# A block with RG-LRU, stick-breaking attention and a squared-ReLU MLP: half of the weight sums made on load by GpSimd, half in memory

## The chip, the cores and the metric

The kernel runs on one core of a Trainium2 chip. The metric is the time of one execution in microseconds (us) of device time, as the median of several runs. PE is TensorE with its weight loads as PEld, DVE is VectorE, ACT is ScalarE, POOL is GpSimd, SP is SyncE, which issues most DMAs.

## The reference

One block of 1024 tokens and 1024 features in float32. The change is about the weights of the MLP: `w_up` is 1024 x 4096 and `w_down` 4096 x 1024.

```python
def hybrid_mixer(h, w_in, ...):
    proj = h @ w_in
    q, k, v, xl, gl = jnp.split(proj, ...)
    q, k = rms_norm per head of 64
    attn = stick_breaking_attention(q, k, v)      # 8 heads, blocks of 128 queries
    xl = causal_depthwise_conv(xl, conv_w, conv_b)
    lru = rg_lru(xl, ...) * gelu(gl)
    return jnp.concatenate([attn, lru], axis=-1) @ w_out

def sq_relu_mlp(h, w_up, w_down):
    return jnp.square(jax.nn.relu(h @ w_up)) @ w_down

def reference(x, ...):
    h = rms_norm(x, norm1_g)
    x = x + hybrid_mixer(h, ...)
    h = rms_norm(x, norm2_g)
    x = x + sq_relu_mlp(h, w_up, w_down)
    return x
```

## The kernel before

**Halves.** Every operand of a large product is kept as two float32r halves: `split` casts the raw tile on ACT (the high part) and subtracts that from the raw tile on DVE or POOL (the low part, line 60). A product then takes three matmuls: low with high, high with low, high with high.

**Stages.** The first 158 us are the norm, the first projections and the recurrence. From 158 to 475 us the list `ORDER` interleaves attention (`A`, for pair of heads, head and block of 256 queries), the projections of the pairs (`O` loads the weights `wr_p` by SP, `I` multiplies, as `pd20` for pair 2 and tokens 0 to 127), the gate of the recurrence (`W` loads `wr_gl`, `G` multiplies) and the weight sums (`Y`). The output projection lasts to 582 us. Then come the two groups of the MLP, g = 0 and 1, each with 2048 of the 4096 hidden features. The code is written in this order, and a scheduler with a model of the engines' times places each engine's instructions before the kernel is built; the order of each engine and queue is then fixed.

**The MLP.** Up and down are each done with seven products of half-size blocks instead of eight (Strassen's scheme). One product is 96 matmuls of 512 columns. On the way up, loop `a` does two products, `s` two, `t` one and `u` two, over eight steps j; the results are the four units `U[:, j, q]`, squared after the ReLU. The way down takes the units in the products p1, p5, p6, p3, p7, p2, p4, each in four steps of 512 KB of weights (`rp`) and two units, some of them subtracted first (`s1`, `s2` on POOL, `s3` on DVE, `s4` into a raw tile). Some products need sums of two to four blocks of a weight matrix.

**The weight sums.** These are made in DRAM, by DMAs that POOL issues: `weight_sum(n)` copies a block of 2 MB or adds one to what is there, and is issued behind the last marked POOL instruction. There are 32 calls: eight for each of u0, d0 (way up and down of group 0), u1 and d1. The first sixteen are the `Y` entries of `ORDER`, the others are issued in the loops of group 0. SP loads the finished sums like any other weights, through three raw tiles of 4 KB a partition (pool `raws`).

**Load of weights in a step.** A step issues the load by SP, then ACT's cast, then the low part on DVE, or for every third one on POOL (`lo_eng`), then PE's matmuls. Stationary tiles have three buffers and moving tiles five.

## Time and profile before

| | before |
|---|---|
| median of 3 runs | 1229.58 us (1226.56 to 1234.42) |
| the profiled execution | 1226.07 us, its span 1224.3 us |
| mean granted clock of PE | 0.977 of full speed |
| PE busy | 1145.2 us, 94% of the span |
| DVE, ACT, POOL busy | 66%, 45%, 46% |
| weight sums issued | 32, the first at 158.46 us |

The span is from the first to the last instruction of the profiled execution; 1.8 us of its time lie around it. The granted clock is what the chip allowed PE, as a share of full speed. Shares of busy time are means over stages with different limits.

### The profile page before, as it was taken

To read this page: it belongs to the slowest core of one execution; us is meant where nothing else is said; L and a number is where in the kernel's file an instruction comes from. 1 tells how busy PE (TensorE), PEld (TensorE's weight loads), DVE (VectorE), ACT (ScalarE), POOL (GpSimd) and SP (SyncE) were. 2 spreads that over 40 slices of the span, in tenths; PEclk is the share of its full clock that TensorE was granted. 3 is DMA by queue.
4 is the path that set the end of the run, shared out by engine and by line. 5 is a ranking of instruction groups with operands and counts; after the bars stand their busy time and mean duration, and the time that the engine had idled before them with its cause. 6 is when DMAs were issued, how large, how long until landed. Compare 5 with 4: busy or idle time off the path is not lost.

```text
span 1224.3 us, 15029 instructions
## 1 busy us (share of the span) xinstructions
PE 1145.2 (94%) x5410; PEld 940.2 (77%) x5410; DVE 804.6 (66%) x1156; ACT 551.4 (45%) x959; POOL 561.4 (46%) x490
## 2 busy tenths in 40 slices
...
GB/s 261 49 47 35 33 162 119 212 194 110 293 105 185 64 208 140 209 1 1 154 274 105 199 240 129 255 240 181 261 63 49 138 89 93 128 109 64 172 104 69
DMA packets 92555, 169.62 MB, mean 139 GB/s; under 512 B 7697, under 2 KB 26177, under 8 KB 92481
## 3 DMA queue, kind: packets, MB, share of 16 engines
q1 hardware_dynamic: 67392, 101.56, 25.8%
q0 software_dynamic: 25088, 67.11, 23.3%
...
HBM read 158.16 MB, written 77.60 MB: 193 GB/s over the span
## 4 chain that ended last, share of the span: by engine, by line
PE 62%; DVE 14%; DMA 8%; issue 7%; POOL 6%; ACT 4%; SPq 0%; ACTq 0%; DVEq 0%; POOLq 0%
PE p L647 19%; PE pa L647 11%; PE pb L647 4%; PE pc L647 4%; DMA wr_p<-in_w_in_dram 3%; PE po L71 3%; PE po L72 2%; PE po L73 2%; DVE g L455 2%; PE pd L72 2%; PE pd L71 2%; PE pd L73 2%; PE av L475 2%; DMA rp<-in_w_down_dram 2%; PE z L446 2%
## 5 line engine op out<-in xcount | busy, mean ns | idle before, releaser
L456 POOL TENSOR_TENSOR w<-w,g 128x128 f32<-128x128 f32 (+3 forms) x96 | 104.8, 1104 | 92.5 <-DVE g L455 35.7
L60 DVE TENSOR_TENSOR ml_p<-rp,mh_p 128x1024 fp32r<-128x1024 f32 x56 | 94.5, 1687 | 74.9 <-ACT mh_p L558 74.7
L675 POOL TENSOR_TENSOR U<-U 128x512 f32<-128x512 f32 x64 | 84.6, 1373 | 74.1 <-ACT U L674 68.0
L455 DVE TENSOR_TENSOR_SCAN g<-g 128x128 f32<-128x128 f32 (+3 forms) x96 | 110.7, 1165 | 3.4 <-ACT g L450 2.3
L71 PE MATMUL pd<-wh_p,hTl 128*128 128x384 f32 x256 | 91.7, 360 | 15.2 <-ACT wh_p L178 6.9
L647 PE MATMUL pa<-mh_p,sl_p 128*128 128x512 f32 x256 | 100.8, 394 | 3.2 <-DVE sl_p L60 3.1
L558 ACT CAST sh_p<-U 128x1024 fp32r<-128x1024 f32 x48 | 50.5, 1052 | 113.5 <-PE pa L647 48.9
L647 PE MATMUL pa<-mh_p,sh_p 128*128 128x512 f32 x256 | 100.3, 392 | 0.0
L647 PE MATMUL pa<-ml_p,sh_p 128*128 128x512 f32 x256 | 100.2, 391 | 0.0
L72 PE MATMUL pd<-wl_p,hTh 128*128 128x384 f32 x256 | 91.0, 356 | 3.8 <-POOL wl_p L60 3.0
L60 POOL TENSOR_TENSOR sl_p<-U,sh_p 128x1024 fp32r<-128x1024 f32 x16 | 42.6, 2665 | 109.7 <-ACT sh_p L558 109.7
L73 PE MATMUL pd<-wh_p,hTh 128*128 128x384 f32 x256 | 88.8, 347 | 0.0
L558 ACT CAST mh_p<-rp 128x1024 fp32r<-128x1024 f32 x56 | 58.8, 1050 | 62.2 <-DMA rp<-in_w_down_dram 29.7
L60 DVE TENSOR_TENSOR sl_p<-U,sh_p 128x1024 fp32r<-128x1024 f32 x32 | 49.2, 1539 | 29.7 <-ACT sh_p L558 29.7
L71 PEld LDWEIGHTS pd<-wh_p,hTl 128*128 128x128 f32 x256 | 49.5, 194 | 20.3 <-ACT wh_p L178 7.8
L60 DVE TENSOR_TENSOR wtl<-pw,wth 128x512 fp32r<-128x512 f32 (+1 forms) x80 | 49.7, 628 | 18.5 <-ACT wth L470 17.9
L647 PEld LDWEIGHTS pa<-mh_p,sl_p 128*128 128x128 f32 x256 | 48.5, 189 | 14.8 <-DVE sl_p L60 4.4
L470 ACT CAST wth<-pw 128x512 fp32r<-128x512 f32 (+1 forms) x80 | 42.8, 546 | 33.6 <-PE pw L466 19.4
L450 ACT ACTIVATE g<-z 128x384 f32<-128x384 f32 (+3 forms) x96 | 47.7, 497 | 20.0 <-PE z L448 13.0
L647 PE MATMUL p<-mh_t,sl_s 128*128 128x512 f32 x128 | 50.5, 396 | 6.6 <-POOL sl_s L60 6.6
L647 PEld LDWEIGHTS pa<-ml_p,sh_p 128*128 128x128 f32 x256 | 48.5, 189 | 10.1
L647 PEld LDWEIGHTS pa<-mh_p,sh_p 128*128 128x128 f32 x256 | 48.4, 189 | 10.2
...
## 6 DMA issues: line engine op xcount, KB each, us to landing
...
sum_d<-in_w_down_dram POOLq DMA_DIRECT2D x12, 2048.0 KB, 14.7
...
sum_u<-sum_u POOLq DMA_DIRECT2D x4, 2048.0 KB, 18.4
...
```

The lines of the kernel that those rows point to most:

```text
L60: ins = eng.tensor_tensor(lo, src, hi.bitcast(F32), op=ALU.subtract)
L71: nc.tensor.matmul(ps, al, bh, start=start, stop=False)
L72: nc.tensor.matmul(ps, ah, bl, start=False, stop=False)
L73: nc.tensor.matmul(ps, ah, bh, start=False, stop=stop)
L446: nc.tensor.matmul(z, qT[hs, h, qr], kL[hs, k0:k0 + kn], start=False, stop=not diag)
L450: nc.scalar.activation(g[:, :kn], z, AF.Sigmoid, scale=-1.0)
L455: nc.vector.tensor_tensor_scan(gr, gr, gr, g[:, kn:kn + 1], op0=ALU.mult, op1=ALU.bypass)
L456: mark(nc.gpsimd.tensor_tensor(w[:, :kn], w[:, :kn], g[:, 1:kn + 1], op=ALU.mult))
L470: nc.scalar.copy(wth[:, :nw], pw[:, :nw])
L558: nc.scalar.copy(hl[0], src)
L647: nc.tensor.matmul(ps, x_, y_, start=start and n == 0, stop=stop and n == 2, skip_group_check=True)
L675: mark(nc.gpsimd.tensor_tensor(c, c, c, op=ALU.mult))
```

## The change

Each group now has four calls of `weight_sum` for the way up and four for the way down, 16 in place of 32: two copies, then two adds, which leave two sums of two blocks in DRAM. The rest is summed after the load: loops `s` and `u` and the products p5, p6 and p4 load two tiles of raw weights or sums, and POOL adds them (`r + q`) ahead of the split. So `u` loads 1 MB of weights a step, and p5, p6 and p4 1 MB. The low parts in these loops all go to DVE (before, every third to POOL); half of the `s1` and `s2` subtractions go from POOL to DVE; the squares of loop `u` go from POOL to ACT. The scratch of the dynamic DMAs (the ring in which the descriptors of POOL's DMAs stand) is given as 4096 where it was 16384 by default, and `raws` has six buffers in place of three. In `ORDER` there are eight `Y` entries in place of sixteen.

```diff
...
@@ -130,35 +130,21 @@
-    sums = {("u", g): dram.tile([4, 8, P, 512], F32, name=f"sum_u{g}") for g in range(2)}
-    sums.update({("d", g): dram.tile([4, 8 * P, 512], F32, name=f"sum_d{g}") for g in range(2)})
+    sums = {("u", g): dram.tile([2, 8, P, 512], F32, name=f"sum_u{g}") for g in range(2)}
+    sums.update({("d", g): dram.tile([2, 8 * P, 512], F32, name=f"sum_d{g}") for g in range(2)})
     def weight_sum(n):
-        m, g = (("u", 0), ("d", 0), ("u", 1), ("d", 1))[n // 8]
-
...
-        dst, src, adds = ((2, block(*first), False), (0, block(*other), False), (2, block(*second), True), (1, block(*first), False),
-                          (3, block(*corner), False), (0, v[2], True), (1, block(*other), True), (3, v[0], True))[n % 8]
+        m, g = (("u", 0), ("d", 0), ("u", 1), ("d", 1))[n // 4]
+        i, k, dst = ((1, 0, 0), (0, 1, 1), (0, 0, 0), (1, 1, 1))[n % 4] if m == "u" else ((1, 1, 0), (0, 0, 1), (0, 1, 0), (1, 0, 1))[n % 4]
+
+        def rows(w):
+            return w.rearrange("j p c -> (j p) c") if len(w.shape) == 3 else w
+
+
+        f = 16 * g + 8 * i
+        src = rows(w_up[k, f:f + 8] if m == "u" else w_down[k, f * P:(f + 8) * P])
         with tc.issue_after(marked[0]):
-            if adds:
-                nc.gpsimd.dma_start(v[dst], src, accum_op=ALU.add, max_dma_last_dim=2048)
-            else:
-                nc.gpsimd.dma_start(v[dst], src, max_dma_last_dim=2048)
+            nc.gpsimd.dma_start(rows(sums[m, g][dst]), src, max_dma_last_dim=2048, **({"accum_op": ALU.add} if n % 4 > 1 else {}))
...
@@ -540,7 +526,7 @@
     xp1 = pool(ctx, "x1")
     x1 = xp1.tile([P, NT, D], F32, name="x1")
     h2 = xp1.tile([P, KC, S], F32, name="h2")
-    rwp = pool(ctx, "raws", bufs=3)
+    rwp = pool(ctx, "raws", bufs=6)
     mvp = pool(ctx, "moving", bufs=5)
     stp = pool(ctx, "stationary", bufs=3)
...
@@ -669,10 +655,13 @@
         def two(w):
             return w.rearrange("a p c -> p a c")
-        def relu2(j, q, src=None, scale=1.0):
+        def relu2(j, q, src=None, scale=1.0, pool=True):
             c = U[:, j, q]
             nc.scalar.activation(c, c if src is None else src, AF.Relu, scale=scale)
-            mark(nc.gpsimd.tensor_tensor(c, c, c, op=ALU.mult))
+            if pool:
+                mark(nc.gpsimd.tensor_tensor(c, c, c, op=ALU.mult))
+            else:
+                nc.scalar.activation(c, c, AF.Square)
...
@@ -690,8 +679,6 @@
                 ps, st = held
                 mm4(ps, st, 1, b21, False)
                 relu2(j - 1, 0, ps)
-                if g == 0 and j % 2 == 0:
-                    weight_sum(15 + j // 2)
             held = cur
         for u in range(2):
@@ -705,7 +692,13 @@
             nc.vector.tensor_tensor(r, hb(1, 1, u), hb(0, 0, u), **sub)
             t3.append(split(lo_eng(), pair(mvp, f"t3{g}{u}"), r))
         for j in range(8):
-            st = station(f"s{g}{j}", two(SU[0:2, j]))
+            r = raw(f"rs{g}{j}")
+            nc.sync.dma_start(r[:, 0], w_up[1, 16 * g + 8 + j])
+            nc.sync.dma_start(r[:, 1], SU[0, j])
+            mark(nc.gpsimd.tensor_tensor(r[:, 0], r[:, 0], r[:, 1], **add))
+            if g == 0 and j % 4 == 0:
+                weight_sum(8 + j // 4)
+            st = split(nc.vector, pair(stp, f"s{g}{j}"), r)
             ps = out_bank(f"p6_{g}{j}")
             mm4(ps, st, 0, t2)
             nc.vector.tensor_tensor(U[:, j, 2], U[:, j, 2], ps, **sub)
@@ -719,14 +712,14 @@
             nc.vector.tensor_tensor(r, hb(1, 0, u), hb(1, 1, u), **sub)
             t4.append(split(lo_eng(), pair(mvp, f"t4{g}{u}"), r))
         for j in range(8):
+            if g == 0 and j % 4 == 2:
+                weight_sum(10 + j // 4)
             if j % 2 == 0:
                 st = station(f"t{g}{j}", two(w_up[1, 16 * g + 8 + j:16 * g + 10 + j]))
             ps = out_bank(f"p4_{g}{j}")
             mm4(ps, st, j % 2, t4)
             nc.vector.tensor_tensor(U[:, j, 1], ps, U[:, j, 3], **sub)
             relu2(j, 1)
-            if g == 0 and j % 2 == 0:
-                weight_sum(20 + j // 2)
         t1 = moving("t1", [hb(0, 1, u) for u in range(2)])
         for u in range(2):
@@ -736,17 +729,23 @@
         for j in range(9):
             cur = None
             if j < 8:
-                st = station(f"u{g}{j}", two(SU[2:4, j]))
+                r, q = raw(f"ru{g}{j}"), raw(f"rv{g}{j}")
+                nc.sync.dma_start(r[:, 0], w_up[0, 16 * g + 8 + j])
+                nc.sync.dma_start(q[:, 0], w_up[1, 16 * g + 8 + j])
+                nc.sync.dma_start(r[:, 1], SU[1, j])
+                nc.sync.dma_start(q[:, 1], SU[0, j])
+                mark(nc.gpsimd.tensor_tensor(r, r, q, **add))
+                st = split(nc.vector, pair(stp, f"u{g}{j}"), r)
                 ps = out_bank(f"p5_{g}{j}")
                 mm4(ps, st, 0, t1)
                 nc.vector.tensor_tensor(U[:, j, 3], ps, U[:, j, 3], **add)
-                relu2(j, 3, scale=-1.0)
+                relu2(j, 3, scale=-1.0, pool=False)
                 cur = (ps, st)
             if held is not None:
                 ps, st = held
                 mm4(ps, st, 1, b22, False)
                 nc.vector.tensor_tensor(U[:, j - 1, 2], ps, U[:, j - 1, 2], **add)
-                relu2(j - 1, 2)
+                relu2(j - 1, 2, pool=False)
             held = cur
...
@@ -761,11 +760,15 @@
             for k in range(0, 8, 2):
                 r = raw(f"r{name}{g}{k}")
-                nc.sync.dma_start(r, src(k))
+                nc.sync.dma_start(r, src[0](k))
+                if len(src) > 1:
+                    q = raw(f"q{name}{g}{k}")
+                    nc.sync.dma_start(q, src[1](k))
+                    mark(nc.gpsimd.tensor_tensor(r, r, q, **add))
+                    if g == 0 and name != "p4" and k % 4 == 0:
+                        weight_sum(12 + (2 if name == "p6" else 0) + k // 4)
                 mv = split(nc.vector, pair(mvp, f"{name}{g}{k}"), r)
-                st = split(lo_eng(), pair(stp, f"{name}{g}{k}"), unit(k))
-                if g == 0 and k % 4 == 2 and name in steps:
-                    weight_sum(24 + 2 * steps.index(name) + k // 4)
+                st = split(nc.vector if len(src) > 1 else lo_eng(), pair(stp, f"{name}{g}{k}"), unit(k))
...
@@ -794,12 +797,12 @@
         def s1(k):
             u = U[:, k:k + 2]
-            mark(nc.gpsimd.tensor_tensor(u[:, :, 2], u[:, :, 2], u[:, :, 3], **sub))
+            (nc.gpsimd, nc.vector)[k // 2 % 2].tensor_tensor(u[:, :, 2], u[:, :, 2], u[:, :, 3], **sub)
             return u[:, :, 2]
         def s2(k):
             u = U[:, k:k + 2]
-            mark(nc.gpsimd.tensor_tensor(u[:, :, 2], u[:, :, 2], u[:, :, 0], **sub))
+            (nc.gpsimd, nc.vector)[k // 2 % 2].tensor_tensor(u[:, :, 2], u[:, :, 2], u[:, :, 0], **sub)
             return u[:, :, 2]
...
@@ -813,23 +816,22 @@
             nc.vector.scalar_tensor_tensor(u[:, :, 2], u[:, :, 2], -1.0, u[:, :, 3], op0=ALU.mult, op1=ALU.subtract)
             return u[:, :, 2]
-        steps = ("p5", "p6", "p3", "p7")
         pa = banks4(QA, "pa")
-        product("p1", pa, wd(0, 0), unit(0), True)
+        product("p1", pa, (wd(0, 0),), unit(0), True)
         acc(pa, 0, 0, rs2)
         pb = banks4(QB, "pb")
-        product("p5", pb, rd(2), s1, True)
+        product("p5", pb, (wd(0, 0), wd(0, 1)), s1, True)
         acc(pb, 1, 1, rs2)
-        product("p6", pa, rd(0), s2, False)
+        product("p6", pa, (rd(0), wd(0, 0)), s2, False)
         acc(pa, 0, 1, nrs2)
-        product("p3", pb, wd(1, 1), s4, False)
+        product("p3", pb, (wd(1, 1),), s4, False)
         acc(pb, 0, 1, rs2, True)
-        product("p7", pa, rd(1), s3, False)
+        product("p7", pa, (rd(0),), s3, False)
         acc(pa, 1, 1, nrs2, True)
         pc = banks4(QB, "pc")
-        product("p2", pc, wd(1, 0), unit(1), True)
+        product("p2", pc, (wd(1, 0),), unit(1), True)
         acc(pc, 0, 0, rs2, True)
-        product("p4", pa, rd(3), unit(3), False)
+        product("p4", pa, (rd(0), rd(1)), unit(3), False)
         acc(pa, 1, 0, rs2, True)
     for g in range(2):
@@ -849,7 +851,7 @@
     from concourse import mybir as _mybir
     from concourse.bass_utils import run_bass_kernel_spmd as _run
-    nc = _bacc.Bacc("TRN2", target_bir_lowering=False, num_devices=1)
+    nc = _bacc.Bacc("TRN2", target_bir_lowering=False, num_devices=1, dynamic_dma_scratch_size=4096)
     arrays, args = {}, []
     for name in _INS:
         a = _np.asarray(inputs[name])
```

**PE, behind the gate's last product of the first pair.** `pgl11` is the gate, `pd20` the projection of pair 2, `av` and `pw` are attention, `z` its scores. Before:

```order
L71 MATMUL pgl11_3139<-hTh_100,wl_gl0_7_2833 128x512
L72 MATMUL pgl11_3139<-hTl_101,wh_gl0_7_2832 128x512
L73 MATMUL pgl11_3139<-hTh_100,wh_gl0_7_2832 128x512
L71 MATMUL pd20_3225<-wh_p2_0_3173,hTl_101 128x384
L72 MATMUL pd20_3225<-wl_p2_0_3174,hTh_100 128x384
L73 MATMUL pd20_3225<-wh_p2_0_3173,hTh_100 128x384
```

After, the rows behind the gate:

```order
L71 MATMUL pgl11_3134<-hTh_100,wl_gl0_7_2829 128x512
L72 MATMUL pgl11_3134<-hTl_101,wh_gl0_7_2828 128x512
L73 MATMUL pgl11_3134<-hTh_100,wh_gl0_7_2828 128x512
L461 MATMUL av013_1799<-wtl0132_1832,vv0_289 128x256
L461 MATMUL av013_1799<-wth0132_1831,vv0_289 128x256
L461 MATMUL av013_1799<-wtl0132_1832,vv0_289 128x256
L461 MATMUL av013_1799<-wth0132_1831,vv0_289 128x256
L452 MATMUL pw0110_1879<-ident_79,w0120_1857 128x128
L452 MATMUL pw0110_1879<-ident_79,w0130_1868 128x128
```

The projection of pair 2 has moved some 80 rows back; attention stands in its place.

**POOL, around the low parts of pair 3's weights in the attention stretch.** `wl_p3` are these, `sum_d0` the sums for the way down of group 0, `kl`, `raw`, `w` and `g` belong to projection and attention. Before:

```order
L161 DMA sum_d0_95<-in_w_down_dram 1024x512 x2
L228 TENSOR_TENSOR raw22_3567<-raw22_3567,qkg_280 128x2x128
L449 MEMSET g2110_3380 128x1
L60 TENSOR_TENSOR wl_p3_0_3951<-wr_p3_0_3949,wh_p3_0_3950 128x384
L456 TENSOR_TENSOR w2000_3330<-w2000_3330,g2000_3329 128x128
L456 TENSOR_TENSOR w2010_3341<-w2010_3341,g2010_3340 128x256
L449 MEMSET g2120_3514 128x1
L60 TENSOR_TENSOR wl_p3_2_3963<-wr_p3_2_3961,wh_p3_2_3962 128x384
L449 MEMSET g2130_3525 128x1
L159 DMA sum_d0_95<-in_w_down_dram 1024x512
L60 TENSOR_TENSOR kl22_3646<-raw22_3567,ks22_3645 128x128 x2
L161 DMA sum_d0_95<-in_w_down_dram 1024x512
```

After:

```order
L442 TENSOR_TENSOR w2100_3365<-w2100_3365,g2100_3364 128x128
L435 MEMSET g204512_3666 128x1
L442 TENSOR_TENSOR w2110_3376<-w2110_3376,g2110_3375 128x256
L214 TENSOR_TENSOR raw22_3561<-raw22_3561,qkg_280 128x2x128
L60 TENSOR_TENSOR wl_p3_0_3944<-wr_p3_0_3942,wh_p3_0_3943 128x384
L60 TENSOR_TENSOR wl_p3_2_3956<-wr_p3_2_3954,wh_p3_2_3955 128x384
L60 TENSOR_TENSOR kl22_3640<-raw22_3561,ks22_3639 128x128 x2
L147 DMA sum_d0_95<-in_w_down_dram 1024x512
L60 TENSOR_TENSOR wl_p3_4_3968<-wr_p3_4_3966,wh_p3_4_3967 128x384
L60 TENSOR_TENSOR wl_p3_6_3980<-wr_p3_6_3978,wh_p3_6_3979 128x384
```

Where two copies, an adding sum and a further copy (and one more behind) stood within these rows, there is one adding sum; the copies that it follows stand 15 and 25 rows ahead of it.

**POOL, end of loop `u` of group 0.** `U` of 128x512 is a square, `U` of 128x2x512 the subtraction `s1`, `sl_` a low part, `ru` and `rp5` raw tiles to which a second one is added. Before:

```order
L675 TENSOR_TENSOR U_6157<-U_6157 128x512 x4
L60 TENSOR_TENSOR sl_u04_7070<-ru04_7067,sh_u04_7069 128x1024
L675 TENSOR_TENSOR U_6157<-U_6157 128x512 x2
L797 TENSOR_TENSOR U_6157<-U_6157 128x2x512
L675 TENSOR_TENSOR U_6157<-U_6157 128x512 x4
L797 TENSOR_TENSOR U_6157<-U_6157 128x2x512
L60 TENSOR_TENSOR sl_u07_7181<-ru07_7178,sh_u07_7180 128x1024
L675 TENSOR_TENSOR U_6157<-U_6157 128x512 x3
L797 TENSOR_TENSOR U_6157<-U_6157 128x2x512
L675 TENSOR_TENSOR U_6157<-U_6157 128x512 x2
```

After:

```order
L662 TENSOR_TENSOR U_6149<-U_6149 128x512 x2
L737 TENSOR_TENSOR ru05_7133<-ru05_7133,rv05_7134 128x1024
L737 TENSOR_TENSOR ru06_7175<-ru06_7175,rv06_7176 128x1024
L800 TENSOR_TENSOR U_6149<-U_6149 128x2x512
L737 TENSOR_TENSOR ru07_7217<-ru07_7217,rv07_7218 128x1024
L767 TENSOR_TENSOR rp500_7422<-rp500_7422,qp500_7424 128x1024
L147 DMA sum_d1_96<-in_w_down_dram 1024x512
L60 TENSOR_TENSOR sl_p100_7285<-U_6149,sh_p100_7284 128x1024
L800 TENSOR_TENSOR U_6149<-U_6149 128x2x512
L767 TENSOR_TENSOR rp502_7461<-rp502_7461,qp502_7463 128x1024
```

The squares are gone, and each step's add stands there; the first add for p5 stands ahead of the first low part of p1.

## Rows read from the trace of the kernel before

**Rows 1.** The page, the two DMA queues that carry data, with packets, MB and the time of the packets as a share of 16 engines over the span. q1 is the queue of SyncE's DMAs, q0 that of GpSimd's.
```profile
q1 hardware_dynamic: 67392, 101.56, 25.8%
q0 software_dynamic: 25088, 67.11, 23.3%
```

**Rows 2.** Busy time in stretches, of the matmuls of the MLP (line 647) alone. Columns: the stretch, its length, busy time of PE and of its weight loads with their instructions, the granted clock of PE, the busy share of the 16 DMA engines (all queues), GB/s. In pairs: the whole MLP of group 0 and of group 1; then by stage, group 0 ahead of group 1: the two products of loop `s`; loop `u` with p1 of the way down; p3 with p7.
```profile
581.87:913.91 332.04, 313.69 (x1345) 256.21 (x1346) 0.97 0.70 192
913.91:1220.16 306.25, 305.23 (x1345) 251.96 (x1343) 1.00 0.31 100
627.99:679.93 51.94, 45.29 (x194) 37.04 (x193) 0.93 0.55 174
958.69:1002.21 43.52, 43.52 (x193) 36.04 (x192) 1.00 0.39 126
701.69:777.81 76.12, 68.39 (x289) 54.86 (x288) 0.98 0.78 196
1023.97:1089.60 65.63, 65.58 (x289) 53.99 (x288) 1.00 0.32 105
...
821.33:870.39 49.06, 45.72 (x194) 37.03 (x192) 0.97 0.87 214
1133.12:1176.64 43.52, 43.52 (x194) 36.04 (x192) 1.00 0.44 148
```

**Rows 3.** What PE waited for in the MLP of group 0 (the four largest but one). Columns: us in total, times, longest.
```profile
PE p L647 <- POOL sl_s L60: 6.6, 1, 6.6
...
PE p L647 <- DVE sl_u L60: 2.4, 1, 2.4
PE p L647 <- POOL sl_u L60: 2.3, 1, 2.3
PE p L647 <- DVE U L742: 1.8, 1, 1.8
```

**Rows 4.** Busy time in stretches, whole engines: the attention stretch from the first sum on, and three pieces of it. Columns: stretch, length, busy time (instructions) of PE, weight loads, DVE, ACT, POOL; granted clock, DMA share, GB/s.
```profile
158.46:475.00 316.54, 288.07 (x1584) 232.96 (x1583) 267.15 (x472) 181.04 (x437) 176.06 (x235) 0.96 0.66 166
220.00:240.00 20.00, 13.46 (x71) 10.56 (x70) 12.49 (x18) 7.20 (x19) 8.32 (x10) 0.91 0.77 245
320.00:340.00 20.00, 11.55 (x45) 9.06 (x43) 9.64 (x19) 5.15 (x14) 6.36 (x8) 0.66 1.09 282
400.00:420.00 20.00, 17.01 (x70) 11.46 (x69) 13.62 (x28) 10.15 (x24) 8.46 (x15) 0.83 0.24 55
```

**Rows 5.** What PE waited for in the attention stretch: the three rows that lead to weights. Columns as in rows 3.
```profile
PE pd L71 <- ACT wh_p L178: 6.9, 2, 5.4
PE pd L72 <- POOL wl_p L60: 3.0, 1, 3.0
...
PE pgl L71 <- POOL wl_gl L60: 1.1, 2, 0.9
```

**Rows 6.** The chain that ended last, its three pieces on weight loads in this stretch. Columns: start, length, what.
```profile
223.33 10.02 DMA wr_p<-in_w_in_dram
...
310.59 21.54 DMA wr_p<-in_w_in_dram
...
391.84 11.82 DMA wr_gl<-in_w_in_dram
```

**Rows 7.** POOL around one weight load: the first two and the last of the five sums that it issued between 302.67 and 317.21 us. Columns: start, length, engine, line, operation.
```profile
302.67 1.57 POOL L161 DMA_DIRECT2D sum_d<-in_w_down_dram  x2
...
317.21 1.30 POOL L161 DMA_DIRECT2D sum_d<-in_w_down_dram  x1
```

**Rows 8.** Two tiles over the whole run: `sum_d` (what POOL spends on issuing a copy, ns min/median/max; us from issue to landing of the tile's DMAs, the SyncE loads from it among them), then `rp`, the raw tiles of the way down (cast, subtraction, us to landing of their 512 KB).
```profile
L161 POOL DMA_DIRECT2D sum_d<-in_w_down_dram x8: 757/796/1350, 302.7 to 812.6; - x8
...
DMA to landing us min/median/max: 3.6/14.7/34.2
L558 ACT CAST mh_p<-rp x56: 1038/1051/1057, 736.8 to 1194.2; 128x1024 fp32r<-128x1024 f32 x56
L60 DVE TENSOR_TENSOR ml_p<-rp,mh_p x56: 1207/1225/4701, 737.9 to 1195.2; 128x1024 fp32r<-128x1024 f32 x56
...
DMA to landing us min/median/max: 3.6/5.0/8.9
```

**Rows 9.** Groups of one line, operation and shape in the MLP, on POOL and ACT. Columns: out<-in shapes, count, busy us, mean ns of one, idle time before and what ended it.
```profile
L675 POOL TENSOR_TENSOR U<-U 128x512 f32<-128x512 f32 x64 | 84.6, 1373 | 74.1 <-ACT U L674 68.0 <-issue 6.0
...
L802 POOL TENSOR_TENSOR U<-U 128x1024 f32<-128x1024 f32 x8 | 25.6, 3198 | 7.9 <-DVE sl_p L60 7.8
...
L808 POOL TENSOR_TENSOR s<-U 128x1024 f32<-128x1024 f32 x8 | 19.2, 2402 | 31.5 <-DVE ml_p L60 23.6 <-DVE sl_p L60 7.8
...
L674 ACT ACTIVATE U<-U 128x512 f32<-128x512 f32 x48 | 29.8, 628 | 47.1 <-DVE U L742 24.1 <-DVE U L726 20.5 <-DVE U L748 2.5
```

**Rows 10.** POOL, then DVE, at the end of loop `u` of group 0. Columns as in rows 7.
```profile
716.30 4.54 POOL L675 TENSOR_TENSOR U<-U 128x512 f32<-128x512 f32 x4
720.30 2.83 POOL L60 TENSOR_TENSOR sl_u<-ru,sh_u 128x1024 fp32r<-128x1024 f32 x1
722.61 2.50 POOL L675 TENSOR_TENSOR U<-U 128x512 f32<-128x512 f32 x2
724.61 2.82 POOL L797 TENSOR_TENSOR U<-U 128x1024 f32<-128x1024 f32 x1
...
719.34 9.18 DVE L60 TENSOR_TENSOR sl_u<-ru,sh_u 128x1024 fp32r<-128x1024 f32 x1 [0.44 <-ACT sh_u L558]
```

12 lines of the change are left out of this document (removed), and 6 rows, old and new, of the table ORDER.

## The prediction

> **What bounds the kernel now.** I read the DMA queues on the page first, then the stretches of TensorE (PE) by stage, then what PE and the chain wait for, and last the prices of the elementwise operations. On the page the two data queues hold the 16 engines 25.8% and 23.3% of the span; at a span of 1224.3 us the 32 weight sums of q0 cost 285 us of all 16 engines [rows 1].
>
> The MLP tells the cost of the sums without a model, since its two groups compute the same with the same instructions, and sums are in flight only in the first. Group 0 takes 332.04 us and group 1 306.25, in which PE is busy for 305.23 at full clock: that is its floor [rows 2]. Of the 25.8 us between them, 8.4 lie in loop `s` (51.94 against 43.52), 10.5 in loop `u` with p1 (76.12 against 65.63), 5.5 in p3 with p7 (49.06 against 43.52): 24.4 in stages that read weights while sums run. In each of them the granted clock of group 0 is under 1 where group 1 has 1.00: a gap is paid once as a wait and once more as a stretch at the lower clock. The gaps end on splits of weights that came late: 6.6 us on `sl_s`, 2.4 and 2.3 on `sl_u` [rows 3].
>
> The attention stretch, from the first sum at 158.46 on, has no twin to compare with. Its chain goes three times through a weight load, of 10.02, 21.54 and 11.82 us [rows 6], and PE waits 6.9, 3.0 and 1.1 us for splits of such weights [rows 5]. Just ahead of the longest, POOL had issued five sums between 302.67 and 317.21 without being held up by the ring of its DMAs, at about 0.8 to 1.6 us a row [rows 7]. But DVE, not PE alone, has to get through this stretch: outside the three pieces it is busy for 267.15 - 35.75 = 231.4 of 256.5 us, 90% [rows 4].
>
> **Fewer sums, attention stretch.** Eight sums stand here instead of sixteen. From above: in the three pieces PE is busy for 42.0 of 60 us, against (288.07 - 42.02)/256.5 = 96% elsewhere, so 15.5 us are lost, and the clocks of 0.91, 0.66 and 0.83 cost about 20 x (0.09 + 0.34 + 0.17) = 12 more: 27. By DVE: 35.75 of 60 us against 54.1 at its 90%: 18.4 that it could do in that time and did not; what PE gains beyond it, DVE can't follow. From below: the three waits of PE, 11 us in sum [rows 5], less some 3 that the new order may cost: 8. I take 18.4, since DVE is the fuller one, less 2: an adding sum now stands behind its own copy on POOL and waits for its landing (14.7 us is the median of the tile, of copies, adds and loads [rows 8]), and the products `w` of the attention queue behind it; between copy and add stand 15 rows of POOL work, more than that landing, so the wait is short. **-16.** The move of in_proj(2) on PE (the first order in the part on the change) costs nothing by itself: PE has the attention's matmuls instead, and 80 rows later its weights have landed. The second order shows the loads of pair 3 with one adding sum behind them where five sums were.
>
> **Fewer sums, MLP group 0.** Eight remain of sixteen, four for u1 and four for d1. All 24.4 us go if what remains hides behind the run-ahead; in proportion to the sums, half stays, 12.2. Behind six raw tiles the loads are issued earlier than behind three, and there are never more than two sums at once, so I take the end near nothing: 3 stay. **-21.4.** Loads themselves grow: 1 MB per j in `u` instead of 0.5, and two tiles a step in p5, p6 and p4. A 512 KB load lands in 3.6 us from issue without sums, 8.9 at most beside them [rows 8], against a step of 5.44 us (four steps a product of 21.76; a product is half of the 43.52 us of rows 2), with three pairs in flight; group 1's loops have a DMA share of 0.32 to 0.44 [rows 2], so doubling the weights in `u` is covered there.
>
> **The adds on POOL.** Per group 8 of 128x512 in `s`, 8 of 128x1024 in `u`, 12 in p5, p6 and p4. Each waits for two loads; behind it on POOL stand the squares of the loop before and the next adds, and ACT's cast and DVE's split of the weights wait for it. POOL's price for 128x1024 is 2.40 us where it has the ports to itself (line 808, mean 2402 ns) and 3.2 among DVE's work (line 802); DVE's is 1.22 (median of the `rp` split), half of it [rows 8, 9]. In exchange POOL gives up 16 squares of 1.37 us in `u`, its third of the splits and half of the s1/s2 subtractions, and half of the issues of sums (0.8 us each for a copy [rows 8]). The squares go to ACT: 0.63 us each [rows 9]; ACT then has a cast of 1.05 and four of these, 3.6 us a step of 5.44: free.
>
> What matters is that the two engines hold each other up: in loop `u` a DVE split took 9.18 us while POOL worked off 12.7 us of its queue (4.54, 2.83, 2.50, 2.82), and PE waited 2.4 us for `sl_u` [rows 3, 10]. So I add up unshared durations of both as if they took turns. p5 before: 4 x 2.40 (s1) + 4 x 1.22 (splits of weights) + four splits of units, a third of them on POOL (2.67 x 1.22 + 1.33 x 2.40 = 6.5) = 21.0 us of 21.76. After: 4 x 2.40 (adds) + 2 x 2.40 + 2 x 1.22 (s1) + 8 x 1.22 = 26.6. That is 4.8 over for p5 and the same for p6: 9.7 a group, 19.4 in all. Loop `u` is about level (16 squares of 1.37 = 21.9 give way to 8 adds, 19.2 alone and 25.6 beside DVE); p4 goes from 4.9 + 6.5 = 11.4 to 19.4. The run-ahead can cover an excess if it starts early: p1 ahead of p5, with 11.4 of 21.76, has 10.4 us free, and the third order shows the first add of p5 ahead of p1's first split on POOL. So most of 9.7 is covered: in group 0 it is in the 3 that stay, in group 1 I give back **+3**.
>
> The rule that speaks most against this part is in the Trainium skill, "SBUF — State Buffer", "SBUF: two separate sides": GpSimd and a VectorE operation with two SBUF inputs hold the shared ports in turns, each for a whole instruction, and "GPSIMD Engine Reference", 4.1, advises VectorE for two-input elementwise work, at half the time. The trace agrees on both (9.18 us for one of 1.22 us behind a row of POOL's; 2.40 against 1.22). By that rule alone, without the run-ahead, the sum would be that of the first rival.
>
> **Sum.** -16 - 21.4 + 3 = -34.4. The profiled execution took 1226.07 us (1224.3 and 1.8 around the span), 3.5 under the median of the three runs: 1191.7 and 3.5 make **1195 us**. Its own range: 27 instead of 16 gives 1184; 8 instead, and a few us more of the 12.2 left, 1208.
>
> **Rivals.** *The ports give it back:* p5 and p6 run at their 26.6 us in both groups: 19.4 instead of the some 6 allowed, 1209. For it: p5 filled 21.0 of 21.76 already; against: p1's room. *Attention gains nothing:* the gaps move to other places, because DVE at 90% sets the pace and the new order is another draw of the scheduler: 16 back, 1211. Both together: 1225. *The small ring:* the change doesn't do what it says of the sums. A quarter of the scratch holds a quarter of the descriptors, and POOL might stand at a second sum until the first has drained; with the large one no such hold is seen [rows 7], and nothing of before shows the small. If each of the 8 adds holds POOL for 10 us, and a third to a half of that reaches PE, it is some 30 us: 1225.
>
> *Slower: POOL's queue starves DVE.* In the order, POOL ends loop `u` of group 0 with adds of 128x1024 in a row, s1 and p5's first add among them, without a square or a PSUM wait between (third order). If DVE's split is caught behind such a row as at 719.34, PE loses what it lost there: 2.4 + 2.3 and 1.8 for U (the last a wait on DVE's next step [rows 3]) and 76.12 x 0.02 = 1.5 by the clock, 8 us. There are four places a group for it (end of `u`, p5, p6, p4), 8 in all: 64 us, 1195 - 6 + 64 = 1253. It turns the result round from the sixth such place on (40.4 / 8 = 5.05).
>
> **How the numbers follow.** Forecast 0.50; ports 0.14; attention 0.12; both 0.06; ring 0.08; starved DVE 0.10. The best of all bounds is 1229.6 - 27 - 24.4 = 1178; the range 1178 to 1224 leaves out the starved DVE and the worse half of the 1225s. A measurement of this kernel tells about 1% from no change, 12.3 us; under 1217.3 are the forecast and nearly all of the two rivals at 1209 and 1211: 0.73; within 1%, both together, the ring and the edges: 0.17; above 1241.9: 0.10.
>
> **What the profile after would show.** Right: loops `s`, `u` and p3 with p7 of group 0 within 3 us of group 1's; q0 at about 12% of 16 engines; no weight load of over 10 us in the attention chain, DVE as busy there in a shorter stretch. Ports: p5 and p6 over 21.76 us in both groups, PE waiting for `ml_p` or `sl_p`, splits of DVE at 3 us and more. Ring: POOL's issues of sums at ten us instead of 0.8 to 1.6. Starved DVE: splits of 5 us and more beside rows of POOL adds, each followed by a PE gap and a stretch at the lower clock. I am wrong outright if group 1, which no sum disturbs, comes out longer than 306 us by more than the ports' 10.

## The result, and the profile after

The changed kernel takes 1215.47 us in the median of four runs (1213.39 to 1218.14), the kernel before 1228.74 beside it: a ratio of 0.9886 (0.9845 to 0.9928). It gained 13.3 us where 34 were forecast. The profiled execution of the changed kernel took 1218.14 us, its span 1216.4, 7.9 less than before; the stages below are compared on the two profiled executions.

The page after: what the data queues carried, as in [rows 1].

```profile
q1 hardware_dynamic: 79040, 122.54, 30.5%
q0 software_dynamic: 12544, 33.56, 11.8%
```

The sums take half of what they took (11.8% of 16 engines, 12 were forecast), and the loads 21 MB more. The MLP of the changed kernel by stretches, of its matmuls alone, columns as in [rows 2]. In pairs, group 0 ahead of group 1: the whole MLP; loop `s`; loop `u` with p1 as there, but p5 and p6 too; p3 with p7.

```profile
566.29:899.01 332.72, 314.79 (x1345) 257.30 (x1345) 0.97 0.58 172
899.01:1212.39 313.38, 307.99 (x1345) 252.78 (x1343) 0.99 0.38 127
613.64:657.16 43.52, 43.52 (x194) 36.05 (x193) 1.00 0.50 160
944.08:987.60 43.52, 43.52 (x194) 36.05 (x193) 1.00 0.36 116
678.92:811.97 133.05, 116.03 (x482) 93.43 (x480) 0.94 0.80 219
1009.36:1125.19 115.83, 111.61 (x482) 90.92 (x480) 0.99 0.42 140
811.97:855.49 43.52, 43.52 (x194) 36.05 (x192) 1.00 0.50 170
1125.19:1168.71 43.52, 43.52 (x194) 36.04 (x192) 1.00 0.55 190
```

Three things are to be read here. The MLP starts at 566.29 us instead of 581.87, 15.6 earlier: that is the attention term. Loop `s`, and p3 with p7, of group 0 now take 43.52 us each, as in group 1, at full clock, as forecast. But group 0 as a whole is no shorter (332.72 against 332.04), because loop `u` to p6 takes 133.05 us where five products at 21.76 take 108.8; and group 1 is 7.1 longer, all of it in the same stretch (115.83). So -15.6 + 0.7 + 7.1 = -7.8.

What PE waited for in the MLP of group 0 (columns as in [rows 3]):

```profile
PE p L633 <- DVE sl_u L60: 8.0, 2, 5.6
PE pa L633 <- DVE sl_p L60: 6.8, 1, 6.8
PE p L633 <- DVE sl_a L60: 4.0, 1, 4.0
```

The waits for `sl_s` are gone, those for `sl_u` have grown from 4.7 to 8.0 us, and one of 6.8 for p6's units (`sl_p`) is new. In the attention stretch, whole engines (columns as in [rows 4], same stretch):

```profile
158.46:475.00 316.54, 298.86 (x1622) 245.69 (x1621) 275.60 (x478) 190.07 (x447) 177.60 (x231) 0.93 0.46 126
```

PE is busy 10.8 us longer in these 316.54 us than before, with 1622 instructions against 1584. Part of that is a lower granted clock, 0.93 against 0.96, so the clock that the prediction's bound of 27 counted as lost did not come back. DVE is busy 8.5 us longer (275.60 against 267.15), 87% instead of 84%. The weight loads are no longer in the list of PE's waits, and the longest one in the chain takes 3.81 us.

POOL of the changed kernel in loop `u` and in p5 of group 0 (columns as in [rows 7], with the idle time before and its cause in brackets), then one row of DVE:

```profile
675.68 1.35 POOL L147 DMA_DIRECT2D sum_u<-in_w_up_dram  x1
...
696.56 1.30 POOL L147 DMA_DIRECT2D sum_u<-in_w_up_dram  x1 [8.83 <-issue]
697.38 2.54 POOL L662 TENSOR_TENSOR U<-U 128x512 f32<-128x512 f32 x2
699.38 5.17 POOL L737 TENSOR_TENSOR ru<-ru,rv 128x1024 f32<-128x1024 f32 x2
704.05 2.79 POOL L800 TENSOR_TENSOR U<-U 128x1024 f32<-128x1024 f32 x1
...
761.68 1.32 POOL L147 DMA_DIRECT2D sum_d<-in_w_down_dram  x1
...
780.98 1.31 POOL L147 DMA_DIRECT2D sum_d<-in_w_down_dram  x1 [12.19 <-issue]
```
```profile
698.13 9.80 DVE L60 TENSOR_TENSOR sl_u<-ru,sh_u 128x1024 fp32r<-128x1024 f32 x1 [0.44 <-ACT sh_u L544]
```

Two rivals of the prediction stand in these rows at once. POOL stood 8.83 and 12.19 us at a second adding sum (the first of each pair had landed 20.6 and 19.0 us after its issue, 0.3 us ahead of the second): the small ring. And right behind the first hold POOL works off what had queued up, 9.5 us of rows without a gap, while a split of DVE takes 9.80 us: the starved DVE.

The kernel before has the same sequence in loop `u` of group 0, with the large ring. POOL's row in [rows 10] starts right behind this issue:

```profile
715.50 1.30 POOL L159 DMA_DIRECT2D sum_u<-sum_u  x1 [8.39 <-issue]
```

This add reads a sum that an earlier add, issued at 693.77, had to complete, and that one landed at 714.78: a hold by the data, as far as the rows show, and not by the ring. So POOL could stand behind a sum before as well, outside the stretch of [rows 7]. In both kernels the row that starves DVE is work that piled up on POOL behind a hold.

### The profile page after: what moved, and what is told of

It is laid out like the page before. It is cut to its first block, busy times and chain, and to the rows that moved or that the text cites. A ratio compares the mean times of both kernels' runs of the same rounds, so it can differ in the third digit from the quotient of the medians.

```text
span 1216.4 us, 15273 instructions
## 1 busy us (share of the span) xinstructions
PE 1150.6 (95%) x5410; PEld 948.0 (78%) x5410; DVE 897.3 (74%) x1182; ACT 568.5 (47%) x991; POOL 586.5 (48%) x472
## 3 DMA queue, kind: packets, MB, share of 16 engines
q0 software_dynamic: 12544, 33.56, 11.8%
## 4 chain that ended last, share of the span: by engine, by line
PE 69%; DVE 13%; issue 8%; DMA 3%; POOL 3%; ACT 3%; SPq 0%; DVEq 0%; ACTq 0%; POOLq 0%
PE p L633 22%; PE pa L633 11%; PE pb L633 5%; PE pc L633 4%; PE pd L71 3%; PE pd L72 3%; PE pd L73 3%; PE po L71 3%; PE po L72 2%; PE po L73 2%; PE av L461 2%; PE z L432 2%; PE pw L452 2%; DVE g L441 2%; DVE sl_u L60 2%
## 5 line engine op out<-in xcount | busy, mean ns | idle before, releaser
L442 POOL TENSOR_TENSOR w<-w,g 128x128 f32<-128x128 f32 (+3 forms) x96 | 99.7, 1044 | 107.7 <-DVE g L441 52.7
L60 DVE TENSOR_TENSOR ml_p<-rp,mh_p 128x1024 fp32r<-128x1024 f32 x56 | 110.3, 1971 | 28.1 <-ACT mh_p L544 28.1
L767 POOL TENSOR_TENSOR rp<-rp,qp 128x1024 f32<-128x1024 f32 x24 | 69.0, 2876 | 70.3 <-DMA qp<-in_w_down_dram 39.8
L60 DVE TENSOR_TENSOR sl_p<-U,sh_p 128x1024 fp32r<-128x1024 f32 x38 | 63.4, 1668 | 30.7 <-ACT sh_p L544 30.7
L737 POOL TENSOR_TENSOR ru<-ru,rv 128x1024 f32<-128x1024 f32 x16 | 43.8, 2769 | 58.9 <-DMA rv<-sum_u 58.8
L662 POOL TENSOR_TENSOR U<-U 128x512 f32<-128x512 f32 x32 | 47.0, 1501 | 32.0 <-ACT U L660 32.0
L436 ACT ACTIVATE g<-z 128x384 f32<-128x384 f32 (+3 forms) x96 | 47.8, 497 | 22.9 <-PE z L434 10.4
L660 ACT ACTIVATE U<-U 128x512 f32<-128x512 f32 x48 | 30.0, 628 | 58.6 <-DVE U L721 31.1
## 6 DMA issues: line engine op xcount, KB each, us to landing
sum_d<-in_w_down_dram POOLq DMA_DIRECT2D x8, 2048.0 KB, 13.3
```

The lines of the kernel that those rows point to most:

```text
L60: ins = eng.tensor_tensor(lo, src, hi.bitcast(F32), op=ALU.subtract)
L436: nc.scalar.activation(g[:, :kn], z, AF.Sigmoid, scale=-1.0)
L442: mark(nc.gpsimd.tensor_tensor(w[:, :kn], w[:, :kn], g[:, 1:kn + 1], op=ALU.mult))
L662: mark(nc.gpsimd.tensor_tensor(c, c, c, op=ALU.mult))
L737: mark(nc.gpsimd.tensor_tensor(r, r, q, **add))
L767: mark(nc.gpsimd.tensor_tensor(r, r, q, **add))
```

## The experiments

Stages are compared by how far they exceed 21.76 us a product (worked out from the starts of their matmuls, `u` up to the first matmul of p1); a group has 14 products, so its floor is 304.6. The last column is the median where there were rounds, else the one run, the profiled one. All other columns are of one execution each.

How much chance is in one execution can be read from the table. Thirteen of these kernels, all but the two of before, the one with no sums at all and the last row, have the same instructions in the same order on PE, DVE, ACT and POOL through the attention stretch, and yet their MLP starts anywhere from 560.4 to 566.7. So up to 6 us of a difference in "MLP starts", and with it in the span, are not the edit's.

| kernel | MLP starts | group 0 | `u` | p5, p6 | `u` of group 1 | p5 of group 1 | span | us |
|---|---|---|---|---|---|---|---|---|
| before | 581.9 | 332.0 | 9.8 | 0, 0 | 0 | 0 | 1224.3 | 1228.7 |
| changed | 566.3 | 332.7 | 12.1 | 1.2, 8.8 | 2.3 | 3.9 | 1216.4 | 1215.5 |
| no sums of group 1 | 562.3 | 322.4 | 9.2 | 3.6, 0.1 | 2.5 | 3.7 | 1202.4 | 1204.2 |
| no sums at all | 554.2 | 319.7 | 8.0 | 3.6, 0.1 | 2.5 | 3.5 | 1191.5 | 1194.1 |
| sums of an eighth | 565.3 | 322.7 | 7.2 | 0, 0 | 2.4 | 3.7 | 1205.6 | 1207.3 |
| ring 8192, five raw tiles | 561.0 | 333.8 | 14.0 | 2.8, 8.0 | 4.6 | 3.9 | 1215.7 | 1220.0 |
| five raw tiles | 566.1 | 335.9 | 12.6 | 2.9, 10.7 | 0.5 | 1.9 | 1217.5 | 1219.5 |
| before, ring and tiles as changed | 594.4 | 331.8 | 20.4 | 0.2, 0.1 | 0 | 0 | 1236.6 | 1238.5 |
| sums spaced | 562.4 | 329.6 | 9.1 | 3.6, 0.1 | 2.4 | 4.2 | 1210.1 | 1211.8 |
| spaced, ACT's order | 562.1 | 325.6 | 2.8 | 4.2, 0 | 0.8 | 3.8 | 1204.3 | 1206.1 |
| changed, ACT's order | 560.4 | 330.9 | 13.6 | 1.2, 0.9 | 0.9 | 4.2 | 1208.1 | 1209.9 |
| spaced, adds on DVE | 561.4 | 328.7 | 8.9 | 0, 0 | 6.6 | 0 | 1207.8 | 1212.0 |
| spaced, both | 561.0 | 326.5 | 7.9 | 0.2, 0.2 | 5.4 | 0 | 1203.5 | 1208.9 |
| changed, adds of the way down on DVE | 566.7 | 327.1 | 11.8 | 2.7, 3.3 | 2.3 | 0 | 1207.4 | 1209.2 |
| all that helped | 560.4 | 308.4 | 0 | 0.5, 0.5 | 3.7 | 0.4 | 1186.3 | **1186.7** |
| the same, without ACT's order | 562.6 | 316.6 | 8.0 | 0, 0.6 | 7.2 | 0 | 1200.4 | 1202.2 |
| all that helped, first sums earlier | 573.6 | 307.6 | 0 | 0, 0.5 | 1.2 | 0 | 1196.1 | 1199.9 |

### Is it the sums that are left?

No sums of group 1 (group 1 reads those of group 0):

```diff
+    sums["u", 1], sums["d", 1] = sums["u", 0], sums["d", 0]
     def weight_sum(n):
+        if n >= 8:
+            return
```

> The changed kernel without the eight sums that are issued in the MLP; group 1 loads the sums of group 0 instead, so its result is another. The lower bound of what sums cost there. Ring and traffic theory: group 0 comes down to group 1's 313.4 us and the 2 to 3 us of its start, 315 to 318; 1199 to 1202 in all. Port theory: group 0 stays above 325 us, 1208 or more.

1204.22 us. Its MLP, group 0, columns as above:

```profile
562.28:884.64 322.36, 310.90 (x1345) 255.10 (x1345) 0.98 0.39 126
```

This lies between the two theories. The eight sums that run beside group 0 cost it 10.4 us (332.72 less 322.36). Even so 18 us over the floor stay, 9.2 of them in loop `u`, with no sum in flight. Is it their bytes, or that POOL has to issue them? The same number of issues, an eighth of the rows (both groups read group 0's sums):

```diff
-            nc.gpsimd.dma_start(rows(sums[m, g][dst]), src, max_dma_last_dim=2048, **({"accum_op": ALU.add} if n % 4 > 1 else {}))
+            few = slice(0, 1024 if n < 8 else 128)
+            nc.gpsimd.dma_start(rows(sums[m, g][dst])[few], src[few], max_dma_last_dim=2048, **({"accum_op": ALU.add} if n % 4 > 1 else {}))
...
-        SU = sums["u", g]
+        SU = sums["u", 0]
...
-        SD = sums["d", g]
+        SD = sums["d", 0]
```

> The changed kernel with the eight sums of group 1 at their places but an eighth of their size (256 KB in place of 2 MB); both groups load the sums of group 0, so the result is another. POOL issues as many DMAs as in the changed kernel, and the engines move an eighth. If bytes make the 10.4 us that these sums cost in group 0 (332.7 against 322.4 without them), group 0 takes 321 to 324 us. If it is the issues on POOL and the order around them, 329 to 334.

```profile
565.28:888.01 322.73, 311.59 (x1344) 255.83 (x1345) 0.98 0.41 132
```

1207.34 us, and group 0 as long as without the sums: it is their size (bytes, and with them the time the ring is held), not the issue of one. And with no sum at all:

```diff
     def weight_sum(n):
+        return
...
-        SU = sums["u", g]
+        SU = [w_up[i, 16 * g:16 * g + 8] for i in range(2)]
...
-        SD = sums["d", g]
+        SD = [w_down[i, 2048 * g + 1024:2048 * g + 2048] for i in range(2)]
...
```

> The changed kernel without any weight sum; raw blocks of the weights are loaded in their place, so the result is another. It tells what is left to gain in the attention stretch. Theory that DVE sets the pace there: the MLP starts within 4 us of where it starts with eight sums (562.3 to 566.3 us in the runs so far), since the sums are hidden. Theory that the sums still cost by half of what sixteen did: it starts 10 us or more earlier, at 552 or less. The MLP as in e3_nosum1, group 0 at 322 us.

1194.07 us. The MLP starts at 554.19, 27.7 us ahead of before: more than the 18.4 read from DVE, and in size the bound of 27 which the prediction had read from PE in its three pieces. In substance it is not that bound, which counted some 12 us for the clock: from 158.46 to 475 us the granted clock is 0.96 without any sum, as it was before. Whole engines in this kernel's attention stretch:

```profile
155.00:450.00 295.00, 283.02 (x1596) 232.54 (x1595) 261.90 (x476) 182.44 (x443) 158.62 (x220) 0.97 0.22 70
```

DVE is busy for 89%, about the 90% of the prediction; in the changed kernel it is busy for 261.08 us of the same stretch. The eight sums that stay there cost 6 to 12 us by this (the kernels with them start the MLP at 560.4 to 566.7). But this is one execution, and without the sums the scheduler also placed the attention's instructions in another order, as it did from before to the changed kernel. What the order and what the sums do was not separated.

### Is it the ring?

Twice the ring, with one raw tile less to make room for it; and the raw tile alone:

```diff
-    rwp = pool(ctx, "raws", bufs=6)
+    rwp = pool(ctx, "raws", bufs=5)
...
-    nc = _bacc.Bacc("TRN2", target_bir_lowering=False, num_devices=1, dynamic_dma_scratch_size=4096)
+    nc = _bacc.Bacc("TRN2", target_bir_lowering=False, num_devices=1, dynamic_dma_scratch_size=8192)
```

> The changed kernel with a scratch of 8192 for the dynamic DMAs, and five raw tiles in place of six to make room for it. In the changed kernel two adding sums of group 1 stand on POOL behind the landing of the one before (idle for 8.8 and 12.2 us), and loop u and product p6 of group 0 are 12.1 and 8.8 us longer than their matmuls. Ring theory: the small scratch makes POOL hold, the two holds go and with them most of this excess; group 0 takes 316 to 321 us in place of 332.7, the kernel about 1200. Port theory: POOL's adds block DVE whatever the ring does; the excess stays within 3 us, about 1215. Traffic theory: the sums in flight delay the loads of raw tiles; two adding sums now overlap, so the excess stays or grows, 1213 to 1220.

1219.99 us, ratio to before 0.9939 (0.991 to 0.9967). No issue of a sum in the MLP is held any more, and loop `u` and p6 still lose 14.0 and 8.0. DVE at the end of its loop `t`, beside 9.4 us of POOL rows from 667.96 on:

```profile
668.35 10.72 DVE L60 TENSOR_TENSOR sl_u<-ru,sh_u 128x1024 fp32r<-128x1024 f32 x1 [0.53 <-DMA ru<-sum_u]
```

> The changed kernel with five raw tiles in place of six and the scratch left at 4096: the control for the run with 8192. Ring and port theory: the holds and the excess stay, group 0 at 331 to 335 us, 1213 to 1219 in all. Traffic theory: a shorter run-ahead makes late loads later, group 0 335 us or more.

1219.49 us, one run. The two kernels have the same instructions in the same order through the whole MLP. With the larger ring group 0 is 2.1 us shorter (333.8 against 335.9), and group 1, where no sum is in flight in either, is 5.3 longer; so the 2.1 can't be told from nothing, and the times are alike too. This bounds less than it seems, as the control holds POOL for only 5.38 and 3.13 us, not for 8.83 and 12.19: what holds of that length cost the changed kernel is not shown. The subtraction that p6's units wait for there stands right behind the one of 12.19 us.

With the larger ring p6 is late without a hold. Among what its units need is a subtraction on POOL, beside operations of DVE without a break:

```profile
767.04 7.85 POOL L805 TENSOR_TENSOR U<-U 128x1024 f32<-128x1024 f32 x1 [1.26 <-DVE sl_p L60]
```

The same subtraction takes 2.40 us at 753.97. With five tiles and the small ring it takes 7.86, and p6 loses 10.7. What the small ring does to the 32 sums of before is another matter:

```diff
-    rwp = pool(ctx, "raws", bufs=3)
+    rwp = pool(ctx, "raws", bufs=6)
...
-    nc = _bacc.Bacc("TRN2", target_bir_lowering=False, num_devices=1)
+    nc = _bacc.Bacc("TRN2", target_bir_lowering=False, num_devices=1, dynamic_dma_scratch_size=4096)
```

> The kernel before with only the memory part of the change: scratch 4096 and six raw tiles, all 32 sums in DRAM as before. Ring theory: POOL, which issued five sums in 15 us with the large scratch, has to stand behind landings; some holds of 5 us and more, and the kernel at 1235 or slower. Theory that the holds are hidden and the traffic of the sums counts alone: 1220 to 1230, loop s and u of group 0 as long as before (8.4 and 9.8 us of excess) or, with more raw tiles, some us shorter.

1238.45 us, one run, its span 12.3 over before's; the MLP starts 12.5 later and is as long as before. One of POOL's holds, and the longest wait of PE in the attention stretch, then in group 0:

```profile
334.72 0.77 POOL L161 DMA_DIRECT2D sum_d<-in_w_down_dram  x1 [10.59 <-issue]
```
```profile
PE pd L72 <- POOL wl_p L60: 17.0, 1, 17.0
...
PE p L647 <- POOL sl_u L60: 13.6, 2, 11.1
```

Here low parts of weights stand behind the held sum on POOL (`wl_p` follows it by 2.7 us), and PE waits; six raw tiles don't make up for it.

### A wait that no rival had: ACT's order

Sums spaced, so that none is called in `u`, p5 or p6 (the edits in loops `a`, `s`, `t` and in the products, in this order). POOL runs ahead of PE, though, and issued the first copy for the way down, called in p3, at 767.02, with PE in p5:

```diff
+                if g == 0 and j in (1, 4):
+                    weight_sum(8 + j // 4)
...
-            if g == 0 and j % 4 == 0:
-                weight_sum(8 + j // 4)
+            if g == 0 and j == 2:
+                weight_sum(10)
...
-            if g == 0 and j % 4 == 2:
-                weight_sum(10 + j // 4)
+            if g == 0 and j == 0:
+                weight_sum(11)
...
-                    if g == 0 and name != "p4" and k % 4 == 0:
-                        weight_sum(12 + (2 if name == "p6" else 0) + k // 4)
...
+                if g == 0 and (name, k) in later:
+                    weight_sum(12 + later.index((name, k)))
...
+        later = (("p3", 0), ("p3", 4), ("p7", 4), ("p2", 4))
```

> The changed kernel, scratch 4096 and six raw tiles, with the eight sums of group 1 issued elsewhere: the copies for the way up in loop a and its adds in loop s and ahead of loop t, those for the way down in p3, p7 and p2, so that none stands in loop u, p5 or p6, where two tiles are loaded a step. Ring theory: no hold of over 3 us on POOL in these three stages; u and p6 of group 0 keep 2 to 4 us of excess as in group 1 (2.3 and 0), group 0 316 to 320 us, about 1200. Traffic theory: the same, 1200. Port theory: the excess of u and p6 stays, 1213 to 1217.

1211.78 us, ratio 0.9862 (0.9824 to 0.9901). p6 is clean and loop `u` still loses 9.1; 8.6 are now lost in `s`, p7 and p2 (2.6, 1.6 and 4.4), beside the sums that were moved there. The kernel with no sums loses 8.0 in `u`, so what does PE wait for in it? Its ACT in loop `u` of group 0, and the longest wait of PE in that group:

```profile
688.53 1.04 ACT L545 CAST mh_p<-rp 128x1024 fp32r<-128x1024 f32 x1 [7.03 <-DMA rp<-in_w_down_dram]
689.48 1.04 ACT L545 CAST sh_u<-ru 128x1024 fp32r<-128x1024 f32 x1
```
```profile
PE p L634 <- DVE sl_u L60: 5.9, 1, 5.9
```

ACT stands 7.03 us at the cast of p1's first weights (`mh_p`), with a cast of loop `u` behind it in its queue. The weights of p1 need a raw tile, and the six hold three pairs of `u`, which come free only as `u` goes on; the cast of `u` behind it then follows without a wait, so its own weights were there. If that is it, queueing p1's cast behind `u`'s last one removes it (the first line stands in loop `u`, behind its split; `casts` holds the split's cast):

```diff
+                ucast[:] = casts
...
-                mv = split(nc.vector, pair(mvp, f"{name}{g}{k}"), r)
+                with tc.issue_after(ucast[0]):
+                    mv = split(nc.vector, pair(mvp, f"{name}{g}{k}"), r)
```

> e2_spaced with one thing added: the casts of p1's weights are queued on ACT behind the last cast of loop u. In the run without the sums of group 1, ACT stood 7.8 us at p1's first cast, whose load had no free raw tile until late, with the cast of u's seventh step behind it. Queue theory: this order makes the long gap of loop u in group 0; its excess falls from 9.1 us to 2 to 4, 1203 to 1206 in all. Port theory: the excess stays at 8 us or more, 1210.

1206.14 us: loop `u` of group 0 goes from 9.1 to 2.8 over, that of group 1 from 2.4 to 0.8. Group 0 as a whole gains 4.0, as p1, p5 and `s` lose a little more. The same edit on the changed kernel as it stands:

> The changed kernel with only the casts of p1 queued on ACT behind those of loop u; sums and adds as they are in it. If the queue made u's 12.1 us of excess there too, it falls to 2 to 4 us and the kernel to 1206 to 1209. If in this kernel it is the adding sums in u (POOL held, then a row of POOL work with a DVE split of 9.8 us behind it), the excess stays at 8 us or more.

1209.85 us, but loop `u` of group 0 keeps 13.6: there the adding sum in the loop, with the late loads and the starved split that go with it, is enough by itself. The loss of p6 (8.8, now 0.9) has moved to p1, which loses 7.7 instead of 2.1, and group 0 is only 1.8 shorter; most of what the span gained, 5.9 of 8.3, lies ahead of the MLP, where the two kernels are alike. Loop `u` is 9.2 over without the sums but with the old order, and 2.8 with the sums spaced and the new order: two causes lie on one another, and either alone keeps PE waiting.

### Who should add?

The adds of `u`, p5, p6 and p4 on DVE, on top of the spaced sums; then together with ACT's order:

```diff
-                mark(nc.gpsimd.tensor_tensor(r, r, q, **add))
+                nc.vector.tensor_tensor(r, r, q, **add)
...
-                    mark(nc.gpsimd.tensor_tensor(r, r, q, **add))
+                    nc.vector.tensor_tensor(r, r, q, **add)
```

> The kernel with the sums issued elsewhere (e2_spaced), and in loop u and in p5, p6 and p4 DVE adds the two raw tiles instead of POOL (1.22 us in place of 2.40 to 3.4 each). Port theory: the operations of the two engines shut each other out, so with POOL nearly empty there the excess of group 1 (2.4 in u, 1.0 in p1, 4.2 in p5) goes under 3 us in sum and that of group 0's u falls from 9.1; 1200 to 1207 us. Rival, DVE's own load: 20 adds a group are 24 us more on DVE, p5 comes to some 20 us of DVE in 21.76 and two s1 on POOL beside it; the excess of p5 and p6 grows and the kernel is at 1214 or more.

1212.0 us, ratio 0.9896 (0.9858 to 0.9934). p5 loses nothing in either group any more, loop `u` of group 1 loses 6.6 instead of 2.4, and 8.6 are lost in p2 of group 0, beside the last of the spaced sums (in flight from 830.86 to 850.64). Neither theory had this: p5 is as the port theory has it, and group 1 loses in `u` what it gains there.

> e2_spaced with both: adds of u, p5, p6 and p4 on DVE, and the casts of p1's weights behind u's on ACT. If port and queue theory both hold, group 0 is within 6 us and group 1 within 3 us of the 304.6 of its 14 products, 1196 to 1202 us. If only the queue counts, 1203 to 1206; if DVE is now too full, 1210 or more.

1208.93 us, ratio 0.9879 (0.9832 to 0.9926): the same pattern, 5.4 in `u` of group 1. On the changed kernel, the second of the two edits alone, so that `u` keeps its adds on POOL:

> The changed kernel with one thing changed: DVE adds the raw tiles of p5, p6 and p4. Port theory: the excess of p1, p5 and p6 in group 1 falls from 4.5 us to under 1, that of group 0 from 10.7 to what the sums cost there, 3 to 6; u stays at 12.1 and 2.3; 1204 to 1209 us in all. Rival, DVE too full: 4 us or more in p5 and p6 of group 1.

1209.18 us. p1 and p5 of group 1 in the changed kernel, whole engines (columns as in [rows 4]):

```profile
1058.62:1103.43 44.81, 42.33 (x179) 34.20 (x177) 44.81 (x22) 17.18 (x18) 32.34 (x11) 0.96 0.40 138
```

And in the kernel with the adds of the way down on DVE:

```profile
1053.90:1094.47 40.57, 39.97 (x176) 32.77 (x175) 35.73 (x28) 17.20 (x18) 19.24 (x5) 1.00 0.49 156
```

With the adds on POOL, DVE is busy without a break through both products although it has six operations fewer (22 against 28): they are held up by POOL's. With the adds on DVE itself it has 4.8 us to spare, and PE runs at full clock. So the ports do give something back in p5, and p1 is no room for it, because DVE is full there too.

### Together

The adds of p5, p6 and p4 on DVE, those of `u` on POOL, ACT's order, and the sums of group 1 called in stages that load one tile a step (loop `a` of both groups, p3, p7 and p2 of group 0, loop `t` of group 1) and no longer in loops `s` and `t` of group 0:

```diff
+                if g == 0 and j in (1, 4):
+                    weight_sum(8 + j // 4)
+                if g == 1 and j in (1, 5):
+                    weight_sum(13 + j // 4)
...
+            if g == 1 and j == 0:
+                weight_sum(15)
...
+                if g == 0 and (name, k) in later:
+                    weight_sum(10 + later.index((name, k)))
...
+        later = (("p3", 0), ("p7", 0), ("p2", 0))
```

> e5_actorder with DVE adding the raw tiles of p5, p6 and p4 (loop u's adds stay on POOL), and the sums of group 1 moved to stages that load one tile a step: copies for the way up in loop a, its adds in p3 and p7, the sums for the way down in p2 and in loops a and t of group 1. Theory from the runs so far: u keeps 2 to 3 us of excess, p5 and p6 under 1, loop s and p2 none; group 0 at 312 to 316 us, group 1 at 308 to 310; 1194 to 1201 us. Rival: DVE is too full in p5 and p6 once POOL's run-ahead is gone, 1204 or more.

1186.71 us (1184.97 to 1190.99), ratio to before 0.968 (0.9637 to 0.9724). Its MLP, group 0 and group 1:

```profile
560.36:868.72 308.36, 307.36 (x1344) 253.25 (x1345) 0.99 0.53 166
868.72:1182.37 313.65, 309.46 (x1345) 253.84 (x1343) 0.99 0.48 147
```

All sixteen sums are still made, and group 0 is within 4 us of its floor, better than any theory had it. POOL issued the two adds called in p3 and p7 at 757.34 and 777.56, with PE in p5 and p6, and p6 loses 0.5 beside them where it lost 8.8 in the changed kernel. Group 1 has three of the sums now and is 9.0 over its floor, 4.3 of them in loop `a` and 3.7 in `u`. Without ACT's order:

> e8_best without the queueing of p1's casts behind those of loop u. Queue theory: u of group 0 has 6 to 9 us of excess again in place of 0.0, and the kernel takes 1192 to 1197. If the sums out of u and the adds of p5 on DVE had already freed it, the excess stays under 2 us and the kernel at 1185 to 1190.

1202.18 us. ACT in loop `u` of group 0 stands again at the same cast, and `u` is 8.0 over:

```profile
696.60 1.04 ACT L546 CAST mh_p<-rp 128x1024 fp32r<-128x1024 f32 x1 [6.56 <-DMA rp<-in_w_down_dram]
```

The order alone is worth 11.9 us of the MLP here, 8.2 in group 0 and 3.6 in group 1 (of 14.1 us of span, the rest lies ahead of the MLP), more than the 7.9 us of span that the change brought. Last, the first four sums moved ahead of the attention stretch, into the recurrence (`weight_sum(c)` behind each of its tiles, with the other four spaced):

> e8_best with the four sums of group 0's way up issued in the recurrence, ahead of the attention stretch, where the DMA engines are idle (tenths of 0 and 1 on the page from 60 to 150 us), and the other four spaced out. Without any sum the MLP began at 554.2 us, with eight in the attention at 561.0 to 566.3. Theory that the price goes with the sums in flight beside weight loads: it begins at 555 to 560 us, 1187 to 1197 in all. Rival: the sums disturb the recurrence as much, 561 or later.

1199.9 us, ratio to before 0.9791 (0.9743 to 0.9839): the MLP starts 13 us later than in the best kernel. All of that is there by the gate's first matmul (185.3 against 172.1 us), and 2.6 of it before the first sum was issued, at 85.64. From that matmul to the MLP it takes 388.3 us with either: with four sums, and another order, it is no shorter than with eight.

## Why the prediction was wrong, step by step

**Attention, -16: right, with luck in it.** -15.6 came, in an execution at the late end: kernels with the same instructions there start the MLP 15.2 to 21.5 us ahead of before. The reason was half right. DVE is busy for about the 90% that was read, but the bound from DVE (18.4) was too low, since 27.7 came without sums; and the eight sums left cost 6 to 12, not the 2 that the step took off. Two errors cancel. Whether it is the missing sums or the new order that saved the time is open.

**MLP group 0, -21.4: wrong; +0.7 came.** `s`, p3 and p7 gained 13.9 of 13.9, as forecast. The step that failed is "so I take the end near nothing: 3 stay". It is off by 22.1 us. What the runs showed in its place are differences between kernels, which need not add up in this one, where causes overlap: the eight sums left cost 10.4, near the 12.2 "in proportion" that the text had set aside (7.4 more than the 3); ACT's order 6.3 in `u` (9.1 to 2.8), of which 2.3 come back in other stages; p1 and p5 over their time 4.6 with no sum of group 1 in flight; the rest of `u` 2.8; loop `a` 1.2.

The argument for "3 stay" was that six raw tiles let loads run further ahead. The tiles had doubled, and so had what a step takes: three pairs are no more steps than three tiles were, and the first load of the next stage waits for one of them while its cast already stands in ACT's queue. The part on the adds looked at what stands behind an add on POOL, and not at what stands behind a cast on ACT that waits for a tile.

**The ports, +3 in group 1: too small; 7.1 came.** The price of 26.6 us for p5 was near: 4.8 over were worked out, and 3.5 to 4.2 are lost in p5 of group 1 in every kernel that adds on POOL there with six raw tiles (1.9 and 3.9 with five). p6 loses next to nothing there, so the rival that took the full price in both products was too dear. The failed step is the cover: "p1 ahead of p5 has 10.4 us free" counted unshared durations of p1's own work, while DVE was busy for all of p1 and p5. Loop `u` "about level" lost 2.3 in group 1, of which ACT's order is 1.6 and not the ports. By the Trainium skill, "GPSIMD Engine Reference", 4.1, elementwise work of two inputs belongs on VectorE; the runs agree for p5 and disagree for loop `u`, where moving the adds to DVE made it worse (2.4 to 6.6).

**The rivals.** *The small ring* is there (8.8 and 12.2 us of holds), at two of the four adding sums in the MLP and at none in the attention stretch. It goes with 12 us of span with 32 sums; in the MLP of the changed kernel its cost is not shown. The price of ten us a hold was right; eight such holds were too many. *Starved DVE*: the mechanism is there, 9.80 us for a split that takes 1.23 just before it, but at one or two places of group 0 and not at eight, and POOL's row behind which it stands follows a hold or the issue of a sum, as it already did before at 715.50. *Attention gains nothing* fell.

**The signs named for "wrong outright"** were group 1 over 306 us by more than ten: 7.1 came, and the sign stayed silent, while the error lay in group 0. The one that spoke was "loops `s`, `u` and p3 with p7 of group 0 within 3 us of group 1's": `u` is 9.8 apart (12.1 against 2.3).

The spread of the runs adds to it: the spans differ by 7.9, the medians by 13.3, as the profiled execution of before was 2.7 under the median of its four runs and that of the changed kernel 2.7 over.

What stays open: how much of the 12.1 us in `u` of the changed kernel belongs to the adding sum's bytes, to its hold and to the starved split, since all three come with that sum; and why p6 lost 8 us with the larger ring too, where its rows show the long subtraction on POOL but no run took it away, and 0.9 with ACT's order, where p1 lost 7.7. It is open too why loop `u` of group 1 got longer with the adds on DVE.
